# Cosine-similarity attention: values and transposes in 64-row tiles, one norm-sum set for Q and K, one product for both heads

## The chip, the cores and the metric

The kernel runs on one core of a Trainium2 chip. It uses five engines that run side by side and meet only at semaphores: TensorE (PE in the profile; its weight loads are PEld), VectorE (DVE), ScalarE (ACT), GpSimd (POOL) and SyncE (SP, which issues most transfers). Matmuls write to PSUM, a memory of eight banks. The metric is the device time of one execution in microseconds; the median of the runs counts.

## What is computed

The inputs Q, K and V have 8 batches of 12 heads, 512 positions and 64 columns, in f32; tau is 0.1.

```python
Q_norm = Q / (np.linalg.norm(Q, axis=-1, keepdims=True) + 1e-10)
K_norm = K / (np.linalg.norm(K, axis=-1, keepdims=True) + 1e-10)
scores = np.einsum('bhqd,bhkd->bhqk', Q_norm, K_norm) / tau
weights = np.exp(scores - np.max(scores, axis=-1, keepdims=True))
weights = weights / (np.sum(weights, axis=-1, keepdims=True) + 1e-10)
return np.einsum('bhqk,bhkd->bhqd', weights, V).astype(np.float32)
```

Scores of normalised rows are between -10 and 10, so the kernel leaves the maximum out and exponentiates directly.

## The kernel before

The 96 heads are worked as 48 pairs (`s`), two heads each. Every step of every pair is an `Op` with a name, an engine and a list of the names that it needs. The function `pair` creates the steps up to the transposed Q and K, `rest` those from the scores to the store, `last` the end of the last pair, `head0` the start of the first. The order on each engine is written out by hand: ORDER holds one string of step numbers for each engine, and each engine works its string from left to right. A step that needs a step of another engine waits on a semaphore, and all that stands behind it on its engine waits too.

The steps of one pair, by their names in the code:

- LD, LV: the loads of Q, K (to `qk`) and V (to `vf`), issued by SyncE. VC: GpSimd's cast of V to bf16 (`vb`), with a column of ones beside each head's 64 columns.
- SQ: squares of Q and K to `sq` (bf16), on GpSimd from the fourth pair on.
- The sums of the squares, per position and head (RED). For K, eight accumulating matmuls with an identity (SSQ, L358) fold 64 columns to 8 in columns 320 to 384 of an output bank, and VectorE reduces these 8 (L365). For Q, from the fifth pair on, VectorE reduces all 64 columns from `sq` (L369). Pairs 43 and 47 (BY_VECTOR) use VectorE for both.
- NEW: 1/sqrt of the sums by two Newton steps on VectorE (L394 to L403), for groups of one, two or four pairs (GROUPS), in a ring of three in the bank `n_ps`.
- SCL (L427): Q and K times these factors, to bf16 `qn`. Q on VectorE, K on GpSimd or, in nine pairs, on VectorE.
- TR (L433): eight transposes of 128x128 into one bank, `t_ps`: four for Q, four for K. EVA (L441): VectorE copies all eight to `qt`, where head 0 lies on rows 0 to 63 and head 1 on rows 64 to 127.
- SCO (L532): the scores of one chunk of 128 keys against 512 queries, for both heads: two matmuls of 64 rows, one on each half of the array's rows. Two buffers of two banks each (`sc_ps`) are used in turn, so the scores of a chunk wait until the exponentials of the chunk two before have been read.
- EXP (L548): ACT turns the chunk's 1024 columns into weights `et` (bf16), four chunks a pair. The first pair does it by halves (L524), the last chunk of the last pair in three pieces (L543).
- PV (L565): 32 matmuls of 128 rows and 65 columns; for each head four groups of 128 queries, each summed over the four chunks. Head 0 goes to the bank `o_ps[0]`, head 1 to `o_ps[1]`. Column 64 is the sum of the weights.
- RCP and NRM (L576, L578): reciprocal and product, per head, as soon as that head's values are complete; then ST, the store.

One chunk, the fourth of pair 43, isn't exponentiated by ACT. `poly` computes it with a polynomial on VectorE and GpSimd (OFF); its scores go to the transposes' bank.

## Time and profile before

| what | value |
|---|---|
| median of 3 runs | 190.27 us (189.93 to 191.8) |
| span of the profiled execution | 190.9 us |
| exponentials of 128x1024 on ACT | 186, busy 171.3 us |
| value matmuls | 1504, busy 72.8 us |
| score matmuls | 374, busy 73.3 us |
| transposes | 376, busy 34.3 us |
| norm-sum matmuls | 384, busy 20.0 us |

A row of a group reads: line, engine, operation, output<-input by the program's names, shapes and count; then busy time of the group in us and the mean of one in ns; then the idle time of the engine just before these instructions, and who ended it. Busy time is the union: instructions that overlap on an engine count once, so it can be less than count times mean. The chain that ended last is followed back from the last instruction, at each step to what released it. In a timeline each row is a run of equal instructions: start, length from the first start to the last end, line, operation and count.

### The profile page before, as it was taken

The numbers are of one execution on the slowest core, as the hardware profiler recorded it, in microseconds if no ns is written. First come the engines' busy times: TensorE is split into PE (matmuls) and PEld (weight loads), VectorE is DVE, ScalarE is ACT, GpSimd is POOL, SyncE is SP. The second block draws the span as 40 slices with busy tenths as digits, with TensorE's granted clock in tenths as the row PEclk, the third lists the DMA queues.
The fourth block names the chain that finished last, engine by engine and source line by source line (L and its number), as shares of the span: only waits on it lengthen the run. The fifth ranks groups of instructions, "written<-read, shape, count | busy, mean of one in ns | idle before, by whom it ended". The sixth has DMA issues, their size and how long they took to land.

```text
span 190.9 us, 6650 instructions
## 1 busy us (share of the span) xinstructions
PE 175.9 (92%) x2705; PEld 109.4 (57%) x2705; DVE 170.2 (89%) x552; ACT 182.7 (96%) x215; POOL 161.8 (85%) x150
## 2 busy tenths in 40 slices
PE   7699699999999999999999999999999899897973
PEld 2355266666656666666566666556656565464642
DVE  2668999999999999999997998999999999988642
ACT  5678999999999999999999999999999999999994
POOL 5397898999999999999999999999999994793000
PEclk9958999999999999999999999999999999999998
DMA  5999999997999599999979999999950414000565
GB/s 162 344 348 349 350 348 372 365 297 250 268 351 337 169 260 320 357 366 369 380 277 272 351 377 364 354 379 384 365 194 5 165 58 165 3 0 3 193 197 165
DMA packets 52446, 50.76 MB, mean 266 GB/s; under 512 B 3136, under 2 KB 52416, under 8 KB 52416
## 3 DMA queue, kind: packets, MB, share of 16 engines
q1 hardware_dynamic: 51984, 50.02, 79.7%
q8 instruction: 21, 0.34, 0.8%
q10 hardware_dynamic: 432, 0.33, 0.5%
q14 instruction: 9, 0.07, 0.1%
HBM read 37.75 MB, written 12.58 MB: 264 GB/s over the span
## 4 chain that ended last, share of the span: by engine, by line
ACT 89%; PE 4%; DMA 3%; DVE 1%; issue 0%; SPq 0%
ACT et L548 88%; DMA qk<-in_Q_dram 3%; PE ops L358 2%; PE scps L521 1%; PE tps L433 1%; DVE qn L427 1%; PE scps L532 0%; SPq L312 0%; ACT et L543 0%; ACT sq L333 0%; ACT ob L608 0%; PE tps L270 0%; DVE qn L261 0%; DVE ob L612 0%; PE ops L593 0%
## 5 line engine op out<-in xcount | busy, mean ns | idle before, releaser
L548 ACT ACTIVATE et<-scps 128x1024 bf16<-128x1024 f32 x186 | 171.3, 1113 | 0.6 <-PE scps L532 0.4
L341 POOL TENSOR_TENSOR sq<-qk 128x1024 bf16<-128x1024 f32 x44 | 83.1, 1896 | 0.1
L532 PE MATMUL scps<-qt 64*128 64x512 bf16 x374 | 73.3, 387 | 6.3 <-ACT et L548 3.3
L565 PE MATMUL ops<-vb,et 128*128 128x65 bf16 x1504 | 72.8, 195 | 1.7 <-DVE ob L578 1.0
L565 PEld LDWEIGHTS ops<-vb,et 128*128 128x128 bf16 x1504 | 55.3, 98 | 30.9 <-issue 18.3
L427 POOL TENSOR_TENSOR qn<-qk,rk 128x512 bf16<-128x512 f32 x38 | 39.5, 1045 | 5.9 <-PE scps L532 3.7
L578 DVE TENSOR_TENSOR ob<-ops,rd 128x256 f32<-128x256 f32 x94 | 38.8, 418 | 0.7
L427 DVE TENSOR_TENSOR qn<-qk,nps 128x512 bf16<-128x512 f32 x56 | 37.2, 677 | 0.7 <-ACT nps L386 0.6
L433 PE MATMUL tps<-ident,qn 128*128 128x128 bf16 x376 | 34.3, 222 | 0.9 <-POOL qn L427 0.3
L441 DVE COPY qt<-tps 128x1024 bf16<-128x1024 bf16 x47 | 32.1, 682 | 0.4 <-PE tps L433 0.4
L532 PEld LDWEIGHTS scps<-qt 64*128 64x128 bf16 x374 | 18.2, 92 | 23.5 <-ACT et L548 9.6
L369 DVE TENSOR_REDUCE nps<-sq 128x8 f32<-128x512 bf16 x46 | 30.8, 682 | 0.8 <-POOL sq L341 0.7
L553 POOL TENSOR_SCALAR vb<-vf 128x512 bf16<-128x512 f32 x48 | 29.7, 630 | 0.1
L433 PEld LDWEIGHTS tps<-ident,qn 128*128 128x128 bf16 x376 | 21.9, 99 | 12.0 <-issue 5.4
L576 DVE RECIPROCAL rd<-ops 128x4 f32<-128x4 f32 x94 | 16.1, 174 | 6.6 <-PE ops L565 5.9
L358 PE MATMUL ops<-sq,ident 128*128 128x64 bf16 x384 | 20.0, 199 | 0.1
L358 PEld LDWEIGHTS ops<-sq,ident 128*128 128x128 bf16 x384 | 15.2, 101 | 4.3 <-issue 2.5
L365 DVE TENSOR_REDUCE nps<-ops 128x8 f32<-128x64 f32 x46 | 10.0, 218 | 0.9 <-PE ops L358 0.7
L394 DVE TENSOR_TENSOR nps<-nps,ys 128x32 f32<-128x32 f32 (+2 forms) x34 | 7.0, 207 | 0.4
L395 DVE SCALAR_TENSOR_TENSOR nps<-nps,ys 128x32 f32<-128x32 f32 (+2 forms) x34 | 7.0, 206 | 0.4
L335 POOL TENSOR_TENSOR sq<-qk 128x512 bf16<-128x512 f32 (+1 forms) x5 | 4.7, 956 | 3.2 <-DMA qk<-in_K_dram 2.8
L524 ACT ACTIVATE et<-scps,xs 128x512 bf16<-128x512 f32 x8 | 4.9, 682 | 0.3 <-PE scps L521 0.3
(66 smaller groups left out, 57.8 us busy)
## 6 DMA issues: line engine op xcount, KB each, us to landing
vf<-in_V_dram SPq DMA_DIRECT2D x48, 256.0 KB, 6.6
qk<-in_Q_dram SPq DMA_DIRECT2D x47, 256.0 KB, 5.5
qk<-in_K_dram SPq DMA_DIRECT2D x47, 256.0 KB, 6.3
out_dram<-ob SPq DMA_DIRECT2D x47, 256.0 KB, 5.7
qk<-in_Q_dram SPq DMA_DIRECT2D x2, 128.0 KB, 2.7
qk<-in_K_dram ACTq DMA_DIRECT2D x2, 128.0 KB, 2.8
out_dram<-ob SPq DMA_DIRECT2D x1, 128.0 KB, 1.7
out_dram<-ob SPq DMA_DIRECT2D x1, 64.0 KB, 1.6
```

Source lines behind the costliest of these rows:

```text
L341: lambda e: e.tensor_tensor(out=sqf, in0=data, in1=data, op=ALU.mult))
L358: last = e.matmul(out=o_ps[bank][:, 320:384], lhsT=ident[:, :], rhs=sq[iqs][:, 8 * w : 8 * w + 8, 8 * k : 8 * k + 8], start=(k == 0), stop ...
L369: lambda e, w=w, dst=dst: e.tensor_reduce(out=dst, in_=sq[iqs][:, 8 * w : 8 * w + 8, :], axis=AX.X, op=ALU.add))
L427: lambda e, w=w, r=r: e.tensor_tensor(out=qn[iqn][:, w].rearrange("p t h d -> p h t d"), in0=qk[iq][:, w].rearrange("p h (t d) -> p h t d" ...
L433: last = e.transpose(t_ps[:, w, t, :], qn[iqn][:, w, t].rearrange("p h d -> p (h d)"), ident[:, :])
L441: lambda e: e.tensor_copy(out=qt[iqt][:, :, :, :].rearrange("p w t x -> p (w t x)"), in_=t_ps[:, :, :, :].rearrange("p w t x -> p (w t x)")))
L532: last = e.matmul(out=sc_ps[:, 2 * b + h, :], lhsT=qt[iqt][64 * h : 64 * h + 64, 1, c, :], rhs=qt[iqt][64 * h : 64 * h + 64, 0, :, :], sta ...
L548: lambda e, c=c, b=b: e.activation(out=et[iet][:, c, :, :], in_=sc_ps[:, 2 * b : 2 * b + 2, :], func=ACT.Exp, scale=math.log(2.0) / UNIT i ...
L553: lambda e: e.tensor_scalar(out=vb[:, iq, :, :, 0:DIM].rearrange("p c h d -> p h c d"), in0=vf[iv][:, :, :].rearrange("p h (c d) -> p h c ...
L565: last = e.matmul(out=o_ps[h][:, 65 * t : 65 * t + 65], lhsT=et[iet][:, c, h, 128 * t : 128 * t + 128], rhs=vb[:, iq, c, h, :], start=(c = ...
L576: lambda e, h=h, grid=grid: e.reciprocal(out=rd[io][:, h, :], in_=grid[:, :, DIM]))
L578: lambda e, h=h, grid=grid: e.tensor_tensor(out=ob[io][:, h], in0=grid[:, :, 0:DIM], in1=rd[io][:, h, :].unsqueeze(2).to_broadcast([128, N ...
```

## The change

Seven things change together, and the order of all engines is written anew.

- Transposes (`tr`): sixteen of 64 rows and 64 columns in place of eight of 128x128, alternating between the two halves of the rows; one step TR in place of two. Each half of the rows writes to a bank of its own (`turned[:, r]`). The copy EVA reads both banks and writes runs of 64.
- Values (`pv`): each matmul of 128 rows becomes two of 64, alternating between the row halves. The two of a couple belong to different heads (`h = r ^ u`) and so write to different banks; the first four steps of a pair cover one half of the sums, the next four the other. The loop runs over chunks first, so that a step needs one chunk's exponentials only. There are 3008 such matmuls. The first matmul into each bank clears it, and all others accumulate.
- Reciprocal and product: one step RCP and one step NRM for both heads. The first value step of the next pair waits for NRM of both.
- Norm sums, from the fifth pair on: one SSQ of eight matmuls with 128 columns for Q and K, into 128 columns of the second transposes' bank (`f_ps`), and one reduction to 16 values. VectorE's reductions from `sq` go.
- The norms and Newton values move from `n_ps` to the first transposes' bank (`norm`), in four slots.
- The shared banks get an order: on TensorE each of TR and SSQ waits for VectorE's reading of the one before (`frees`). On VectorE, marks "+n" in its string say between which steps the transposes of a pair may run: they wait for the last step ahead of the mark that touches the norms' bank, and the next such step waits for them (`share`).
- OFF becomes empty: ACT does all chunks, 187 exponentials of 128x1024.

```diff
+    def share(self, order, windows):
+        free = []
+        for o in order["pe"]:
+            if o.frees:
+                o.needs, free = o.needs + free, o.frees
+        last, open_ = None, []
+        for i, o in enumerate(order["dve"]):
+            for w in windows.get(i, []):
+                if last is not None:
+                    w.needs = w.needs + [last.key]
+                open_.append(w.key)
+            if o.norms:
+                o.needs, last, open_ = o.needs + open_, o, []
...
+    o_ps = nc.alloc_psum_tensor("ops", [128, 2, 512], f32)
+    nt_ps = nc.alloc_psum_tensor("ntps", [128, 2, 512], f32)
...
+                    last = e.matmul(out=f_ps, lhsT=ident[:, :], rhs=sq[iqs][:, :, 8 * k : 8 * k + 8], start=(k == 0), stop=(k == 7))
...
-            def tr(e, w=w):
-                for t in range(NT):
+        def tr(e):
+            for j in range(2 * NT):
+                for r in range(2):
+                    rows = slice(64 * r, 64 * r + 64)
                     last = e.transpose(
-                        t_ps[:, w, t, :], qn[iqn][:, w, t].rearrange("p h d -> p (h d)"), ident[:, :])
+                        turned[:, r, 64 * j : 64 * j + 64],
+                        qn[iqn][rows, j // NT, j % NT].rearrange("p h d -> p (h d)"), ident[rows, rows])
...
+        free = [("NRM", s - 1)] if s else bank_free
+        for u in range(2):
+            for i, c in enumerate(turn):
+                def pv(e, u=u, c=c, i=i):
+                    for t in range(NT):
+                        for r in range(2):
+                            rows, h = slice(64 * r, 64 * r + 64), r ^ u
+                            last = e.matmul(
+                                out=o_ps[:, h, 65 * t : 65 * t + 65],
+                                lhsT=et[iet][rows, c, h, 128 * t : 128 * t + 128], rhs=vb[rows, iq, c, h, :],
+                                start=(u == i == t == 0), stop=(u == 1 and i == NT - 1), skip_group_check=True)
...
-OFF = {(43, 3): ((43, 43), "A")}
+OFF = {}
...
-BY_VECTOR = (43, 47)
+BY_VECTOR = ()
...
-RINGS = (17, 9, 6, 4, 4, 5, 8, 3)
+RINGS = (17, 9, 6, 4, 4, 5, 8)
+SLOTS = 4
```

In the head, the new list of TensorE puts the four score matmuls of the first pair's head 0 one behind the other, ahead of the norm sums and of head 1's transpose of Q. A filler matmul of 256 columns goes. ACT's list moves one normalising exponential of the first pair ahead of the squares of the second pair's Q, and an exponential between these squares and the next.

## The prediction

> **What bounds the kernel now.** I read the page first: the shares of the engines and the chain of work that ended last.

> ```profile
> span 190.9 us, 6650 instructions
> ...
> PE 175.9 (92%) x2705; PEld 109.4 (57%) x2705; DVE 170.2 (89%) x552; ACT 182.7 (96%) x215; POOL 161.8 (85%) x150
> ...
> ACT 89%; PE 4%; DMA 3%; DVE 1%; issue 0%; SPq 0%
> ```

> Four engines are over 85% busy, but the chain lies on one of them, ScalarE (ACT). Next, the chain piece by piece (start, length, what).

> ```profile
> 18.15 116.56 ACT et L548 x127
> ...
> 134.74 22.11 ACT et L548 x24
> ...
> 156.86 10.27 ACT et L548 x11
> ...
> 167.14 11.14 ACT et L548 x12
> ...
> 178.29 7.96 ACT et L548 x9
> ...
> 186.46 0.68 ACT et L543
> ```

> From 18.15 on, the kernel is 183 exponentials one behind the other. The longest unbroken piece gives the rate: 116.56 / 127 = 0.918 us for each. At that rate 183 take 168.0 us; from 18.15 to 186.46 there are 168.3. [...] The rest of what can be won lies ahead of it, in the ACT timeline of the head:

> ```profile
> 8.40 1.24 ACT L524 ACTIVATE et<-scps,xs 128x512 bf16<-128x512 f32 x2
> 10.34 0.31 ACT L383 ACTIVATE ys<-xs,eps 128x16 f32<-128x16 f32 x1 [0.69 <-DVE xs L365]
> ...
> 14.09 0.69 ACT L524 ACTIVATE et<-scps,xs 128x512 bf16<-128x512 f32 x1 [0.31 <-PE scps L521]
> 15.18 9.49 ACT L548 ACTIVATE et<-scps 128x1024 bf16<-128x1024 f32 x10 [0.40 <-PE scps L532]
> ```

> Once the exponentials have begun, ACT idles 0.69 + 0.31 + 0.40 = 1.40 us in brackets, and no more.

> **The change, part by part.**

> *The polynomial chunk goes back to ACT.* OFF becomes empty, so the list has 187 full exponentials where it had 186. Nothing covers ACT: +0.92 us, with one answer. VectorE and GpSimd lose that chunk's arithmetic, which isn't on the chain.

> *Row tiles on TensorE.* The groups that the diff touches, and a stretch of the PE timeline:

> ```profile
> L532 PE MATMUL scps<-qt 64*128 64x512 bf16 x374 | 73.3, 387 | 6.3 <-ACT et L548 3.3
> L565 PE MATMUL ops<-vb,et 128*128 128x65 bf16 x1504 | 72.8, 195 | 1.7 <-DVE ob L578 1.0
> ...
> L433 PE MATMUL tps<-ident,qn 128*128 128x128 bf16 x376 | 34.3, 222 | 0.9 <-POOL qn L427 0.3
> ...
> L358 PE MATMUL ops<-sq,ident 128*128 128x64 bf16 x384 | 20.0, 199 | 0.1
> ```

> ```profile
> 104.21 0.40 PE L433 MATMUL tps<-ident,qn 128*128 128x128 bf16 x4
> 104.54 0.39 PE L532 MATMUL scps<-qt 64*128 64x512 bf16 x2
> 104.86 0.66 PE L565 MATMUL ops<-vb,et 128*128 128x65 bf16 x16
> 105.45 0.39 PE L532 MATMUL scps<-qt 64*128 64x512 bf16 x2
> 105.80 0.41 PE L358 MATMUL ops<-sq,ident 128*128 128x64 bf16 x8
> ```

> A run's length less one matmul's own time, over the starts between, is the pitch: values (0.66 - 0.195) / 15 = 31 ns for 65 columns, transposes (0.40 - 0.222) / 3 = 59 ns for 128, norm sums (0.41 - 0.199) / 7 = 30 ns for 64. The two score matmuls lie on 64 rows each; both together last 0.39 where one lasts 0.387, so the two row halves run at once. By the transposes' rate 512 columns need 0.24 us, yet the values start 0.32 after the scores: about 0.09 us is lost. It is lost again on the way back: the sixteenth value matmul starts at 104.86 + 0.66 - 0.195 = 105.33, the next could start at 105.36, the scores start at 105.45. So each change between 64-row and 128-row work costs some 0.09 us.

> Need of a pair before: 4 scores of 0.32 = 1.28, 4 changes into them of 0.09 = 0.36, 32 values of 31 ns = 0.99, 8 transposes of 59 ns = 0.47, 8 norm sums of 30 ns = 0.24: 3.34 us of the 4 x 0.918 = 3.67 that ACT takes. That is 91%, which fits the page's 92%.

> After, 64-row tiles carry the scores, values and transposes; only the norm sums stay at 128 rows. No trace here shows short 64-row matmuls in a row, so I bound them. Both halves at once, as with the scores: 4 scores of 0.24 = 0.95, 32 pairs of value matmuls at 31 ns = 0.99, 8 pairs of transposes at the 30 ns of 64 columns = 0.24, 8 norm sums of 128 columns at 59 ns = 0.47, two changes = 0.18: 2.83 us, 77% of ACT's time. Halves behind each other: 64 x 31 ns and 16 x 30 ns in place of the 0.99 and 0.24, 4.06 us, which is 0.39 more than ACT's 3.67. I take the first, since the score row is the one row of 64-row work there is. [...] The instruction count rises from 2705 matmuls to 4600; what isn't shown is whether they can be issued that densely for long, and that is the doubt in my chance for this.

> The 0.5 us of TensorE that a pair wins sits under ACT. It buys only the 0.3 to 0.6 us of late scores: -0.35.

> *VectorE.*

> ```profile
> L578 DVE TENSOR_TENSOR ob<-ops,rd 128x256 f32<-128x256 f32 x94 | 38.8, 418 | 0.7
> L427 DVE TENSOR_TENSOR qn<-qk,nps 128x512 bf16<-128x512 f32 x56 | 37.2, 677 | 0.7 <-ACT nps L386 0.6
> ...
> L441 DVE COPY qt<-tps 128x1024 bf16<-128x1024 bf16 x47 | 32.1, 682 | 0.4 <-PE tps L433 0.4
> L369 DVE TENSOR_REDUCE nps<-sq 128x8 f32<-128x512 bf16 x46 | 30.8, 682 | 0.8 <-POOL sq L341 0.7
> ...
> L576 DVE RECIPROCAL rd<-ops 128x4 f32<-128x4 f32 x94 | 16.1, 174 | 6.6 <-PE ops L565 5.9
> ...
> L365 DVE TENSOR_REDUCE nps<-ops 128x8 f32<-128x64 f32 x46 | 10.0, 218 | 0.9 <-PE ops L358 0.7
> ```

> Q's 46 reductions go: -30.8. The remaining 44 read 128 elements instead of 64; (682 - 218) / 448 = 1.04 ns an element makes each 285 ns: 12.5 for 10.0, +2.5. Forty-seven reciprocals of about 180 ns for 94: -7.6. Forty-seven products of 512 elements at L427's 677 ns: 31.8 for 38.8, -7.0. The transposes' copy now writes runs of 64; its 682 ns may stay, or at 1.04 ns an element reach 1.2 us, +25 at most. VectorE comes to about 127 of 170 us, 152 at the worst. All of it lies under ACT: nothing.

> *One output accumulator for both heads.* The next pair's first value matmul now waits for reciprocal and product of both heads: 0.2 + 0.18 + 0.68 us plus handovers, some 1.15 us behind the last value matmul. In the new PE list nearly always one or two chunks of scores with a norm sum or a transpose stand between, each chunk released 0.92 us after the last. In four places there is one chunk alone or little more. Behind the waiting matmul stand the next scores; I price those four places at 0.3 us at most each and take +0.3 in all. Before, this wait was per head, so it is a new one.

> *Shared banks.* Transposes, norm sums and norms lie in two banks, so transposes wait for VectorE's last touch of them, norm sums wait for the copy, and VectorE's next touch waits for the transposes. Behind a waiting transpose stand the values and scores; behind VectorE's stand its Newton steps and products. Slack at the scores:

> ```profile
> 17.72 0.39 PE L532 MATMUL scps<-qt 64*128 64x512 bf16 x2
> ```

> Scores that start at 17.72 release the exponential at 18.15, 0.43 later; a buffer is free one exponential earlier, 0.92, and exponentials overlap by about 0.1. So TensorE may be 0.35 to 0.4 us late without ACT noticing. VectorE idles a third of the time, so I price these waits at nothing; without that cover, see below.

> *The head.* Here TensorE sets the pace, and slowly. The windows for 9 to 18 us (busy time of PE, PEld, DVE, ACT, POOL, then the granted clock), and VectorE's copy for pair 2 in the timeline:

> ```profile
> 9.00:18.00 9.00, 8.93 (x98) 5.27 (x98) 6.73 (x26) 7.59 (x14) 8.64 (x8) 0.64 1.10 349
> ```

> ```profile
> 17.83 0.69 DVE L441 COPY qt<-tps 128x1024 bf16<-128x1024 bf16 x1
> ```

> PE 8.93 busy of 9.00 at a granted clock of 0.64. The new list puts the four first scores together, ahead of the norm sums, moves one normalising exponential into ACT's wait for the second pair's Q, and halves the length of the first pair's transposes. That lets pair 1 start earlier. But pair 2's scores still stand behind the copy (17.83 before), behind two Newton chains on VectorE. So the head wins between nothing and the 1.40 us of idle time, and could lose 0.5 if that copy moves back. I take -0.5, a third.

> The tail (last pair, stores) keeps its instructions: nothing.

> **Sum.** +0.92 - 0.35 + 0.3 - 0.5 = +0.4 us against the profiled 190.9: 191.3. The median of the runs is 190.27, 0.6 below the profiled span, so the forecast is 190.27 + 0.4 = 190.6. From its bounds (head -1.4 to +0.5, late scores -0.6 to 0, accumulator 0 to +1.2) it runs from about 189.2 to 192. Inside that case I lean low, 190.4, as VectorE's relief also speeds the Newton chains of the head.

> **Rivals.**

> *The head closes altogether.* All 1.40 and 0.6 us go and nothing new comes: 190.27 + 0.92 - 2.0 = 189.2; a head that keeps its full clock, run by run, might give 0.5 more, 188.7. For: TensorE is the head's bound. Against: pair 2's copy. That is as fast as ACT's work allows. Chance 0.09, a third of it beyond 1%.

> *Row halves don't overlap in short matmuls, and TensorE becomes the bound.* Fully serial: 0.39 us a pair over some 44 pairs, +17, 207. It decides from the point where the 80 matmuls of a pair start 26 ns apart on average ((3.67 - 0.95 - 0.47 - 0.18) / 80). Just under that, at 25 ns, the mean still fits (3.60 of 3.67), but the list puts up to 48 of them between two scores, 1.2 us where 0.68 plus the 0.4 of slack fit: one such place in every three or four pairs loses 0.1 to 0.4 us, so +3 to +6, 193.5 to 196.5. For it: twice the instructions. Against it: the score pairs. [...] Chance 0.14.

> *Lockstep.* TensorE and VectorE, each in order, hand two banks back and forth twice a pair. If a transpose finds VectorE still ahead of its window by more than the 0.4 us of slack, ACT stops. One tenth of a us in each of 44 pairs is +4.4: 194.8; from 0.04 us a pair (1.9 / 44) it is measurable. For: both lists are fixed and six waits a pair are new. Against: PE at 77% and VectorE at two thirds. Chance 0.18.

> **How the numbers follow.** Forecast 0.59, the head's rival 0.09, serial halves 0.14, lockstep 0.18. Range: 188.9 to 196.0; it leaves out the fastest 0.04 and the 0.12 or so beyond 196. A difference of 1% (1.9 us) is about what a measurement here can tell from none. Faster by over 1% takes the best head: 0.04. Slower: serial halves, lockstep without its mildest part and a little of the forecast's edge, 0.32. Within: 0.64.

> **What would show it.** Right: 187 exponentials at 0.918 us without breaks, PE's share near 80% with value matmuls starting in pairs some 4 ns apart and pairs about 31 ns apart, no gap between scores and values, VectorE near two thirds. Wrong: value matmuls 25 to 31 ns apart singly, or a chain that leaves ACT for PE's transposes and VectorE's copy each pair. The forecast would be wrong most easily in the head, where 0.5 us is a choice between 0 and 1.4.

## The result and the profile after

The changed kernel takes 210.84 us (median of four runs, 207.2 to 217.06) beside 190.23 for the kernel before on the same chip: a ratio of 1.094, with a 95% interval of 1.083 to 1.105. The ratio isn't the quotient of the two medians, because it leaves out two of the four executions, the profiled one among them, that took over 1.5% longer than the fastest. The profiled execution has a span of 209.6 us. It belongs to a run of 211.6 us, so it stands close to the median.

The page of the kernel after: the shares of the engines (busy time, share of the span, instructions), TensorE's granted clock and the DMA engines' busy share in 40 slices, the queue that brings instructions, the chain that ended last, and four groups.

```profile
span 209.6 us, 10353 instructions
...
PE 168.5 (80%) x4600; PEld 111.3 (53%) x4600; DVE 142.9 (68%) x407; ACT 186.0 (89%) x216; POOL 156.8 (75%) x146
...
PEclk9969999999999999999995799969988999999999
DMA  5999999950699997796499189889567967413333
...
q8 instruction: 36, 0.59, 1.3%
...
ACT 28%; PE 25%; DVE 16%; POOL 9%; DMA 9%; issue 8%; SPq 2%; POOLq 1%; DVEq 0%
...
L583 ACT ACTIVATE et<-scps 128x1024 bf16<-128x1024 f32 x187 | 174.5, 1074 | 17.1 <-PE scps L567 16.6
L374 POOL TENSOR_TENSOR sq<-qk 128x1024 bf16<-128x1024 f32 x44 | 83.1, 1896 | 15.1 <-DMA qk<-in_K_dram 14.0
...
L603 PE MATMUL ops<-vb,et 64*128 64x65 bf16 x3008 | 75.1, 193 | 10.4 <-issue 6.1
L588 POOL TENSOR_SCALAR vb<-vf 128x512 bf16<-128x512 f32 x48 | 29.5, 628 | 7.5 <-DMA vf<-in_V_dram 7.4
```

TensorE is busy 80% and VectorE 68%, close to the 77% and two thirds forecast, but partly by luck: these are shares of a span that is 19 us longer. In the last control below, with a span of 193.4 us, they are 84% and 74%. ACT now holds 28% of the chain instead of 89%, and its exponentials stood 16.6 us for scores. Two things on this page were not in the prediction. The value matmuls stood 6.1 us for "issue", that is, for nothing that the profile shows. GpSimd's squares stood 14.0 us for K's loads. The instruction queue carried 36 packets; before it was

```profile
DMA  5999999997999599999979999999950414000565
...
q8 instruction: 21, 0.34, 0.8%
```

(the DMA row is that of the kernel before, in slices of 4.8 us). Each packet is 16 KB (0.59 MB / 36). In both traces TensorE has two instructions for a matmul, a weight load (PEld) and the matmul: 2 x 4600 = 9,200 now and 2 x 2705 = 5,410 before. 36 x 256 = 9,216 and 21 x 256 = 5,376, so both traces come to some 256 instructions a packet.

Where the time went can be counted on ACT. The last full exponential ends at 205.30 us instead of 186.65. The first one starts 1.56 earlier, one more costs 0.92, and between first and last there are 23 breaks of over 0.15 us, 19.6 us in sum; before there was one, of 0.2. (A break is what an exponential ends later than 0.918 us after the one before it.) I put each break to what came before it on TensorE: 9.9 us follow a stop in the middle of a step, 7.5 follow a late load, 1.6 are the head, 0.6 other.

A stop in the middle of a step, in the PE timeline of the kernel after (start, length, what, idle time before it and its releaser):

```profile
109.01 0.23 PE L603 MATMUL ops<-vb,et 64*128 64x65 bf16 x3 [0.16 <-DVE ob L617]
111.42 0.32 PE L603 MATMUL ops<-vb,et 64*128 64x65 bf16 x5 [2.18 <-issue]
111.53 0.64 PE L567 MATMUL scps<-qt 64*128 64x512 bf16 x2
```

Three value matmuls of a group of eight run, the other five 2.4 us later, with no semaphore between. The DMA queues from 108.9 to 110.0 us (packets, MB, share of 16 engines' time) show one instruction packet among loads that fill the engines:

```profile
q1 hardware_dynamic: 391, 0.37, 101.8%
q8 instruction: 1, 0.02, 5.0%
```

That packet moved from 109.03 to 109.91. The windows show what follows (PE, PEld, DVE, ACT, POOL busy, granted clock, DMA share, GB/s):

```profile
104.00:109.00 5.00, 4.43 (x152) 2.90 (x146) 4.14 (x9) 5.00 (x6) 3.20 (x4) 1.00 0.99 315
109.10:111.40 2.30, 0.14 (x3) 0.02 (x4) 0.06 (x1) 1.05 (x2) 2.30 (x4) 0.89 1.04 353
111.40:117.00 5.60, 5.58 (x87) 3.70 (x88) 1.19 (x4) 3.11 (x4) 4.47 (x5) 0.50 0.64 221
```

In the 5.6 us after the stop the granted clock is 0.50, and ACT works 3.11 of them: the stop is paid more than once. There are eight such stops of over 0.43 us, 10.0 us in sum, and all lie at the same place in TensorE's own count of instructions: at 192 above a multiple of 256.

The late loads, in the chain from 142 to 156 us, and SyncE's list (SPq) in the timeline:

```profile
143.13 6.28 DMA qk<-in_K_dram
149.41 0.07 issue
149.48 1.35 POOL sq L374
...
155.25 0.61 PE ntps L470 x16
155.86 0.85 PE scps L567 x4
```

```profile
44.46 0.37 SPq L351 DMA_DIRECT2D vf<-in_V_dram  x1
53.12 0.38 SPq L621 DMA_DIRECT2D out_dram<-ob  x1
53.55 1.27 SPq L348 DMA_DIRECT2D qk<-in_Q_dram  x2
```

A load of K asked for at 143 lands 6.28 us later, and GpSimd squares pair 41 behind it. In GpSimd's list these squares stand ahead of the scaling of pair 36's K, so that pair 36's transposes and scores come last. At 53 us SyncE had stood 8.3 us at a store that waited for its product, with loads behind it in its list. From pair 9 on, each store of pair s stands directly ahead of V of pair s + 9 and Q, K of pair s + 12; in the list before, the stores stood among the loads of Q and K of pairs some 12 to 21 ahead. When the store goes, the loads go in a burst.

### The profile page after: what moved, and what is told of

It reads as the page before. It is cut to its first block, busy times and chain, and to the rows that moved or that the text cites. A ratio compares the mean times of both kernels' runs of the same rounds, so it can differ in the third digit from the quotient of the medians.

```text
span 209.6 us, 10353 instructions
## 1 busy us (share of the span) xinstructions
PE 168.5 (80%) x4600; PEld 111.3 (53%) x4600; DVE 142.9 (68%) x407; ACT 186.0 (89%) x216; POOL 156.8 (75%) x146
## 4 chain that ended last, share of the span: by engine, by line
ACT 28%; PE 25%; DVE 16%; POOL 9%; DMA 9%; issue 8%; SPq 2%; POOLq 1%; DVEq 0%
ACT et L583 28%; PE ops L603 8%; PE scps L567 8%; PE ntps L408 5%; DVE ob L617 5%; DMA qk<-in_K_dram 5%; POOL sq L374 4%; PE ntps L470 3%; DVE qt L478 3%; DMA qk<-in_Q_dram 3%; DVE qn L462 2%; POOL vb L588 2%; POOL qn L462 2%; DMA vf<-in_V_dram 2%; SPq L348 2%
## 5 line engine op out<-in xcount | busy, mean ns | idle before, releaser
L583 ACT ACTIVATE et<-scps 128x1024 bf16<-128x1024 f32 x187 | 174.5, 1074 | 17.1 <-PE scps L567 16.6
L603 PE MATMUL ops<-vb,et 64*128 64x65 bf16 x3008 | 75.1, 193 | 10.4 <-issue 6.1
L603 PEld LDWEIGHTS ops<-vb,et 64*128 64x128 bf16 x3008 | 62.3, 96 | 30.5 <-DVE ob L617 10.3
L478 DVE COPY qt<-ntps 128x1024 bf16<-128x1024 bf16 x47 | 32.3, 687 | 22.5 <-PE ntps L470 22.4
L462 DVE TENSOR_TENSOR qn<-qk,ntps 128x512 bf16<-128x512 f32 x56 | 36.8, 680 | 0.3
L617 DVE TENSOR_TENSOR ob<-ops,rd 128x512 f32<-128x512 f32 x47 | 32.4, 689 | 1.5 <-DVE ys L442 0.3
L408 PE MATMUL ntps<-sq,ident 128*128 128x128 bf16 x352 | 28.6, 226 | 1.2 <-DVE rd L615 0.4
L470 PE MATMUL ntps<-ident,qn 64*128 64x64 bf16 x752 | 20.4, 194 | 10.1 <-POOL qn L462 5.9
L408 PEld LDWEIGHTS ntps<-sq,ident 128*128 128x128 bf16 x352 | 20.9, 100 | 11.6 <-issue 6.5
L470 PEld LDWEIGHTS ntps<-ident,qn 64*128 64x128 bf16 x752 | 15.5, 97 | 16.6 <-issue 7.9
L388 DVE TENSOR_REDUCE ntps<-ntps 128x16 f32<-128x128 f32 x44 | 13.0, 295 | 14.9 <-PE ntps L408 14.7
L433 DVE TENSOR_TENSOR ntps<-ntps,ys 128x32 f32<-128x32 f32 (+2 forms) x34 | 7.1, 208 | 0.7
```

The source lines that it names most:

```text
L388: lambda e: e.tensor_reduce(out=dst, in_=in_, axis=AX.X, op=ALU.add)).norms = not acts
L408: last = e.matmul(out=f_ps, lhsT=ident[:, :], rhs=sq[iqs][:, :, 8 * k : 8 * k + 8], start=(k == 0), stop=(k == 7))
L462: lambda e, w=w, r=r: e.tensor_tensor(out=qn[iqn][:, w].rearrange("p t h d -> p h t d"), in0=qk[iq][:, w].rearrange("p h (t d) -> p h t d" ...
L470: last = e.transpose(turned[:, r, 64 * j : 64 * j + 64], qn[iqn][rows, j // NT, j % NT].rearrange("p h d -> p (h d)"), ident[rows, rows])
L478: lambda e: e.tensor_copy(out=qt[iqt][:, :, :, :].rearrange("p w t (r x) -> p r (w t) x", r=2), in_=turned.rearrange("p r (k x) -> p r k x ...
L583: lambda e, c=c, b=b: e.activation(out=et[iet][:, c, :, :], in_=sc_ps[:, 2 * b : 2 * b + 2, :], func=ACT.Exp, scale=math.log(2.0) / UNIT i ...
```

## The experiments

Three theories. F: TensorE's instructions come in blocks of 256, whose packets pass through DMA engines that the loads keep full (101.8% of them in the window above); 1.7 times the instructions (9,200 for 5,410) use a block up before the next is there. L: loads come late because each stands behind a store. K: TensorE and VectorE in lockstep, at the shared banks (the prediction's rival "Lockstep") or at the one output accumulator. Times are medians; each ratio is to the kernel before, with its interval.

**Values in 128-row form** (3,096 matmuls instead of 4,600; the cut is abridged):

```diff
-                        for r in range(2):
-                            rows, h = slice(64 * r, 64 * r + 64), r ^ u
-                            last = e.matmul(out=o_ps[:, h, ...], lhsT=et[iet][rows, c, h, ...], rhs=vb[rows, iq, c, h, :], ...)
+                        last = e.matmul(out=o_ps[:, u, ...], lhsT=et[iet][:, c, u, ...], rhs=vb[:, iq, c, u, :], ...)
```

> The changed kernel with its values back in matmuls of 128 rows (1504 for 3008; the first four steps of a pair are head 0, the next four head 1), everything else as changed, the order of the engines too. PE's instructions fall from 9200 to about 6200. Theory F (TensorE is starved of instructions: its stream comes in blocks of 16 KB, 256 instructions, and the changed kernel uses a block up before the next has come): the stops of 1.2 to 2.4 us in the middle of a step go, ACT's idle time of 17 us falls below 6, and the time to 191 to 196 us, though the scores pay 0.19 us for each change of form again. Theory L (SyncE's list puts each store in front of loads, so the loads come late and GpSimd, then TensorE, wait): GpSimd's 14 us of waiting for K stay, time 203 or more. Theory K (lockstep of TensorE and VectorE at the shared banks): the order is the same, PE has less slack, time 207 or more.

207.31 us, ratio 1.084 (1.075 to 1.094). Not one stop in the middle of a step is left, but the loads are as late, as its waits say (us, times, longest):

```profile
POOL sq L374 <- DMA qk<-in_K_dram: 12.5, 13, 2.9
```

ACT's breaks fall from 19.6 to 14.1 us. F's time, 191 to 196, is missed; 207.31 lies where L and K had it. So the stops go with the additional instructions, and removing them alone wins little: the loads stay late and the changes of form come back.

**Stores later** (row halves kept; from pair 8 on each store takes the place of the store four pairs later in SyncE's list, of which this is a piece, LD standing for the loads of Q and K):

```diff
- ... ST.12 LV.21 LD.24 ST.13 LV.22 LD.25 ...
+ ... ST.8  LV.21 LD.24 ST.9  LV.22 LD.25 ...
```

> The changed kernel with SyncE's list altered alone: the store of each pair from the eighth on stands where the store of the pair four later stood, so that loads are issued up to four pairs (15 us) earlier. L: GpSimd's waits for K and V (14.0 and 7.4 us) go and the time falls to 192 to 197. F: the stops in the middle of a step stay (about 10 us of PE in all), the time falls only where late loads had added to them: 199 to 205. K: no change, 207 to 211.

209.1 us (204.0 to 211.4). GpSimd's waits for loads are gone but for the first pairs; the stops grow from 8 to 12 and from 10.0 to 18.0 us. The PE timeline and the waits:

```profile
56.77 0.33 PE L603 MATMUL ops<-vb,et 64*128 64x65 bf16 x10
59.25 0.51 PE L603 MATMUL ops<-vb,et 64*128 64x65 bf16 x22 [2.15 <-issue]
```

```profile
PE ops L603 <- issue: 13.1, 10, 2.5
```

The time lies in K's range and misses F's (199 to 205) and L's (192 to 197). L alone falls: what the loads stop losing, the blocks lose. I put that down to SyncE, which now keeps the DMA engines full for longer.

**Light loads** (row halves and list kept; the output differs; abridged):

```diff
+    out=qk[iq][0 : 128 if s < R_QK else 32, w], in_=src(x, s)[0 : 128 if s < R_QK else 32]
+    out=vf[iv][0 : 128 if s < R_V else 32, :, :], in_=src(V, s)[0 : 128 if s < R_V else 32]
```

> The changed kernel with the loads of Q and K from pair 17 on and of V from pair 9 on cut to 32 of 128 partitions; the rest of each buffer keeps an earlier pair's values, so the output is another. The same instructions and orders, but a quarter of the load traffic from some 30 us on. F: a block of instructions still needs its own microsecond and more, but no longer stands behind data; the stops become fewer or shorter, time 192 to 202. L: loads land at once, though issued as late as before: 198 to 205. K: no change, 207 to 211.

197.12 us, ratio 1.029 (1.021 to 1.037), as F had it. The program on TensorE is the same to the instruction, and the stops fall to two, one of them while the loads are still whole. So the stops hang on the traffic too.

**Values in 128-row form and stores later**, both edits above:

> Both edits: values in 128 rows and stores four pairs later. F with L as its consequence: as the first, 191 to 194. L as a cause of its own: clearly below each of the two alone. K: 205 or more.

200.65 us, ratio 1.050 (1.045 to 1.056). Neither F's time (191 to 194) nor K's (205 or more) was right. It is clearly below each of the two edits alone, as L as a cause of its own had it. There is no stop and, after the first pairs, no wait for a load, and yet the time is 10 us more than before. ACT has 29 breaks, 28 of them of 0.15 to 0.4 us, 8.3 us in sum. The chain that ended last, and the longest wait, with the same wait before:

```profile
PE 42%; DVE 26%; ACT 18%; POOL 8%; issue 4%; DMA 1%; DVEq 0%
```

```profile
PEld ops L601 <- DVE ob L615: 16.5, 42, 1.0
```

```profile
PEld ops L565 <- DVE ob L578: 5.7, 17, 0.9
```

My reading: with changes of form at every change of step, 0.11 us each by the next run, TensorE has too little slack for the wait at the common accumulator. So here the waits point to the part of K that concerns the accumulator. No run takes the common accumulator out, and that the shared banks cost time as well isn't shown.

**Half the chunks' values in 128-row form**, stores later (abridged):

```diff
+                        if i % 2:
+                            last = e.matmul(out=o_ps[:, u, ...], lhsT=et[iet][:, c, u, ...], rhs=vb[:, iq, c, u, :], ...)
+                            continue
```

> Two of a pair's four chunks give their value matmuls back to 128-row form and two keep the 64-row halves; stores stand four pairs later in SyncE's list, as in the run with later stores. 7,696 TensorE instructions instead of 9,200. F (instruction blocks come too late): a block of 256 lasts 6.3 us on average instead of 5.3 us, so the stops inside steps at block boundaries, 12 with 18.0 us in the run with later stores and all row halves, become fewer: 0 to 5, under 6 us in sum; 199 to 206 us. If the row halves themselves are too slow on TensorE (serial or contending), the stops don't depend on the number of instructions and the time is half way: about 204.9 us with as many stops in the 64-row chunks as there were.

211.37 us, ratio 1.105 (1.097 to 1.113). A miss in time. The stops did as F says: none is left that a late packet explains, where there were twelve. But 63% of the chain is TensorE, and its timeline tells why:

```profile
82.84 0.29 PE L609 MATMUL ops<-vb,et 64*128 64x65 bf16 x8
83.07 0.30 PE L602 MATMUL ops<-vb,et 128*128 128x65 bf16 x4
83.30 0.30 PE L609 MATMUL ops<-vb,et 64*128 64x65 bf16 x8
83.53 0.29 PE L602 MATMUL ops<-vb,et 128*128 128x65 bf16 x4
83.75 0.39 PE L567 MATMUL scps<-qt 64*128 64x512 bf16 x2
```

Four couples take 0.12 us by themselves, and a group starts every 0.23: each change of form costs 0.11 us. My mixture changes form inside a step. From 60 to 160 us its trace has 223 changes, the 128-row form with later stores 185: 9.1 and 7.1 a pair, 0.22 us apart by that price, and the pairs are 4.06 and 3.86 us long.

**Paced loads.** All bytes and row halves; each load waits for an exponential some pairs earlier, so that transfers are spread. Three versions of the lead, and the 128-row form with the first two (abridged; D and DV are the leads in pairs):

```diff
+        for c, k in enumerate([("LD", p + D, 1), ("LD", p + D, 0), ("LV", p + DV)]):
+            P.ops[k].needs.append(("EXP", p, c if (p, c) not in OFF else c + 1))
```

> All row halves kept, all bytes moved. The loads of Q and K of pair p + 10 and of V of pair p + 5 wait for the exponentials of pair p, one load for each of its first three, and the store of pair p - 2 stands behind them: SyncE then issues four transfers spread over each pair rather than in bursts, and loads run at most 10 pairs ahead instead of 17. F with its queue (a block's packet waits 2 to 4 us behind loads when the DMA engines are full, and a block is used up in 5.3 us): from about 45 us on the engines aren't full at the request, the packet starts within about 1 us, stops inside steps fall from 12 (later stores) or 8 (the change) to 3 at most, all before 45 us, and no squares wait for a late load: 193 to 198 us. L alone (only late loads matter): the waits for loads go, the stops stay: 204 to 210 us. Instruction number alone, whatever the traffic: stops stay, 204 to 210 us. K (lockstep at the shared banks): neither moves, 205 us or more.

> Values in 128-row form in all chunks and the same paced loads: 6,192 TensorE instructions, 256 of which last 8 us. F: there was no stop to remove, and no load came late with later stores, so pacing brings nothing: 199.5 to 201.5 us, like values in 128-row form with later stores (200.65 us). If pacing helps by something other than the blocks and the late loads (less contention on the buffers), it is below 198 us here too.

232.67 and 237.45 us, ratios 1.222 (1.210 to 1.234) and 1.238 (1.225 to 1.251): both misses by my choice of V's lead. GpSimd scales V up to six pairs ahead and V was asked for five ahead, as the waits of the first show:

```profile
POOL vb L588 <- DMA vf<-in_V_dram: 40.2, 17, 6.3
```

Of the stops they say little; the first still has seven with 8.1 us, five of them after 50 us, where F had forecast none. With longer leads:

> The paced loads again with longer leads: Q and K of pair p + 13 and V of pair p + 8 wait for the exponentials of pair p. In the first paced run V came only five pairs ahead, while GpSimd scales V up to six pairs ahead, so GpSimd stood 40.2 us for V; this is mended here. All row halves and all bytes stay. F with its queue: while the rings fill, to about 55 us, the DMA engines are full and two to four stops of 1 to 1.5 us remain; after that a block's packet starts within 2 us of the request, and there is at most one stop of over 1 us. With the waits for loads under 3 us: 195 to 200 us. If the number of instructions alone makes the stops, or the queue is as full with pacing as without: 5 or more stops after 60 us and 203 us or more. If GpSimd still waits over 10 us for loads, the run says something of the stops only.

> Values in 128-row form with the same paced loads and longer leads: no stops to remove, and load waits that later stores had removed already. F and L: 199.5 to 201.5 us, as with later stores (200.65 us), so that the paced row halves come out faster than the paced 128-row form. If pacing helps through something else, such as less traffic on the buffers, both paced kernels gain alike and this one is below 198 us.

206.69 us (ratio 1.085, 1.074 to 1.097) and 200.58 us (1.053, 1.043 to 1.063). The second is as F and L say. The first misses its 195 to 200 us. Its stops moved as forecast in part: after 57 us there are three with 2.7 us, one of them over 1 us, but before, while the rings fill, six with 8.3 us, where two to four were forecast. Its DMA engines in 40 slices of 5 us:

```profile
DMA  5999999999977888999969979989858445113333
```

They are full up to 55 us, and again later: pacing spreads the bursts, but Q, K, V and the output of a pair keep the engines near full in any case.

> Paced loads once more, all row halves and all bytes kept: the lead of Q and K grows from 9 pairs to 12 and that of V from 4 to 8, so that fewer bytes are asked for before pacing begins. In the paced run with longer leads five of the six stops of over 0.5 us before 60 us were in the stretch in which the DMA engines filled the rings (7.0 us of stops, 8.6 us of late exponentials), one after it. F with its queue: the stretch is shorter, the stops between 40 and 60 us go, two to three remain before 40 us (2 to 4 us in sum); with no load later than its user the time is 195 to 201 us, below 202 us and below the paced 128-row form or equal to it. If the stops between 40 and 60 us stay though the engines are not full there, the queue is not their cause and the time is 203 us or more.

205.52 us (201.34 to 207.31). Another miss: fewer stops before 40 us (one instead of three), more after, ten with 10.7 us in all, each at a place where the DMA engines were 78% busy or more between the block's boundary and the packet. None of these versions of pacing is the cure.

**Two controls.** The kernel before with light loads, and the change with light loads and later stores:

> The kernel before with the same cut as the light loads: from pair 17 Q and K, from pair 9 V load only 32 of their 128 partitions (the rest keeps what the buffer held, so the output differs). A control: if light traffic speeds the kernel by something other than the blocks and the late loads, this one falls too, by 2 us or more. F and L: ScalarE's exponentials bound it and its blocks have 3.3 us to spare under full traffic, so nothing moves: 189.5 to 191.5 us.

> Light loads as in the run of that name (197.12 us) and the stores four pairs later as well, row halves kept; the same part of the loads is left out. GpSimd's 8 us of waits for loads, which were left there, go. Of the late exponentials (4.0 us from the third to the last) 2.0 us lay at 26 us and before, where the traffic is still full, and some 1.2 us behind waits for loads after 140 us. F and L: 195.5 to 197.5 us. Lockstep at the shared banks would leave breaks in each pair whatever the loads do, and the rate of the exponentials between 30 and 185 us would be above 0.93 us; F and L say 0.92.

The kernel before doesn't move: 190.31 us, ratio 0.999 (0.995 to 1.003). The change comes to 195.93 us, ratio 1.029 (1.020 to 1.038), also as forecast, and its chain reads like that of the kernel before:

```profile
37.77 31.32 ACT et L583 x34
```

```profile
73.82 61.75 ACT et L583 x67
```

61.75 / 67 = 0.922 us for each exponential: row halves, shared banks and one accumulator cost ACT next to nothing when instructions and data are there. K falls for this form. Its breaks over 0.15 us are six with 3.1 us, all but one before 38 us.

**The blocks in all traces.** I took every boundary of 256 TensorE instructions (192, 448, ... in its count) in seven kernels with row halves throughout: the change, later stores, both with light loads, and the paced ones. For each I compared the end of the next block's packet with the last instruction before the boundary.

```
boundaries                                                  245
packet ended later than 1.3 us before the boundary     about 77
  of these with a stop of over 0.43 us                       50
packet ended earlier, with a stop of over 0.43 us             0
from the packet's end to the next instruction, in a stop    1.0 to 1.6 us, median 1.4
```

At the 92 boundaries of the four kernels with values in 128-row form, and at the 20 of the kernel before, no packet was that late. The rates say why. With row halves a block lasts 5.0 us on average (3.4 at the shortest; from the control with light loads and later stores), in the kernel before 8.4 (7.3 at the shortest). Against it stand the packet's start after the previous boundary (median 0.8 us where the DMA engines were under 30% busy, 3.4 and up to 6.6 where they were over 90%, counted in the kernels with row halves but for that control; at most 3.7 in the kernel before), about 1 us for the packet, and 1.4 us until it is executed. That makes 3.2 us when the engines are free and, by the medians, 5.8 when they are full: row halves fit the first and not the second, and the kernel before, with 6.1 at the most, fits both.

## Why the prediction was wrong

The forecast was 190.4 us, with a range up to 196.0; the measured time is 210.84. Two terms that the sum doesn't have, late instruction blocks and late loads, stand for 17.4 of ACT's 19.6 us of breaks. A third, the head, is in the sum with the wrong sign.

**What bounds the kernel now.** Right: 183 exponentials at 0.918 us. The kernel before with light loads, which leaves the time where it was, agrees. Of the late scores' 0.6 us the profile of before shows 0.3 (168.3 against 168.0 us); the other 0.3 no run shows.

**The polynomial chunk.** Right as a term: 187 exponentials, at 0.92 us.

**Row tiles on TensorE.** The mechanism held. In the PE timeline after, 24 value matmuls last 0.54 us:

```profile
60.00 0.54 PE L603 MATMUL ops<-vb,et 64*128 64x65 bf16 x24
60.42 0.39 PE L567 MATMUL scps<-qt 64*128 64x512 bf16 x2
```

(0.54 - 0.19) / 23 = 15 ns, so a couple takes 30 ns; its halves mostly start 3 to 11 ns apart. The change of form was priced at 0.09 us and measured 0.11. The halves do overlap, so the rival of serial halves, 0.14, is out. The 4 ns that the prediction expected within a pair are near the score couples of the trace of before, whose halves start 3 to 6 ns apart. The 25 ns from matmul to matmul, at which it put the rival's lower end, was a trial value under its own 26: no run shows a limit there.

What failed is the sentence that closes this step: "what isn't shown is whether they can be issued that densely for long, and that is the doubt in my chance for this". I saw the doubt and priced it only as a pitch of matmuls, within the rival "Row halves don't overlap in short matmuls". The limit here is not the pitch but the supply: 9,200 instructions in blocks of 256, whose packets start 3.4 us after the boundary where the DMA engines are over 90% busy and 0.8 us where they are under 30% (the medians above). The page of before had both rows (21 instruction packets, and DMA engines at 9 tenths in most slices up to 140 us); I used neither. The supply had no term in the sum. In the profile after it stands for 9.9 us of breaks.

**Loads.** There was no term for them either. I followed the order of TensorE and ACT through the change and not SyncE's list, in which each store now stands directly ahead of the loads of pairs nine and twelve ahead: 7.5 us of breaks. In the 128-row form, where there are no stops, moving the stores won 6.7 us (207.31 to 200.65). With row halves the two terms feed each other: moving the stores alone won nothing beyond the spread of the runs (209.1, from 204.0 to 211.4), cutting the traffic won 13.7, and both 14.9 of the 20.6.

**VectorE.** Priced at about 127 us in work and nothing in time; its busy time is 142.9, under ACT all the same. The working took groups' busy times off the engine's, but instructions of different groups overlap: VectorE's groups add up to 203 us before, where the engine is busy for 170.2. The copy into runs of 64 takes 687 ns, so the feared +25 didn't come. Nothing in time, as forecast, outside the head, where TensorE isn't stopped and has slack.

**One output accumulator** (+0.3) **and shared banks** (nothing). Small, as forecast, with row halves: 0.922 us an exponential in the last control. In the 128-row form (200.65 us) the accumulator's wait grows, to 16.5 us, once changes of form use TensorE's slack up; I had not seen that the two parts of the change depend on each other in this way. The rival Lockstep, 0.18 at 194.8 us, meant the shared banks, and no run shows that these cost time by themselves.

**The head** (-0.5). This term has the wrong sign. ACT's timeline after:

```profile
13.62 1.95 ACT L583 ACTIVATE et<-scps 128x1024 bf16<-128x1024 f32 x2
16.01 2.14 ACT L583 ACTIVATE et<-scps 128x1024 bf16<-128x1024 f32 x2 [0.43 <-PE scps L567]
18.88 3.81 ACT L583 ACTIVATE et<-scps 128x1024 bf16<-128x1024 f32 x4 [0.73 <-PE scps L567]
```

The first full exponential starts 1.56 us sooner than the 15.18 of the profile before, and 1.58 us of breaks follow by 18.9, at pair 1's and pair 2's scores. The fifth starts at 18.88, beside 19.07 in that profile, so the head seems to win 0.2 us. But the profile before is of an execution whose head ran at a granted clock of 0.64, and its span of 190.9 us is 2.5 above 188.4, the median of the thirteen spans on record beside the two controls. The prediction took the 1.40 us of idle time in that head for the kernel's own. In the control of the kernel before, whose loads are the same up to 22 us, the clock is full and ACT has no such break (a window, then ACT's timeline):

```profile
9.00:18.00 9.00, 7.91 (x119) 4.75 (x118) 8.41 (x32) 9.00 (x15) 8.70 (x9) 1.00 1.10 355
12.67 10.19 ACT L548 ACTIVATE et<-scps 128x1024 bf16<-128x1024 f32 x11
```

There the fifth full exponential starts at 16.28. With the changed order and row halves throughout it starts at 17.6 to 17.9 in the four traces whose clock from 9 to 18 us was 1.00 as well (later stores and the three paced ones), and at 18.5 to 18.9 in the other three, whose clock there was 0.81. So the head loses 1.4 to 2.6 us, more than the 0.5 that the prediction allowed for. The prediction had named the place: pair 2's scores stand behind the copy, which starts at 14.96 in the control of the kernel before and at 16.46 with later stores:

```profile
14.96 0.69 DVE L441 COPY qt<-tps 128x1024 bf16<-128x1024 bf16 x1
```

```profile
16.46 0.68 DVE L478 COPY qt<-ntps 128x1024 bf16<-128x1024 bf16 x1
```

What is left without late blocks and late loads, 195.93 us, is 5.6 us above the kernel before on that chip (190.35). Between the traces of the two controls ACT's last full exponential ends 5.3 us apart, at 189.15 and 183.83. Of these, 2.6 are there by the fifth exponential, 0.92 is the added exponential, and 1.35 are breaks after the two stops that remain while the rings fill; the other 0.4 are one more break and the rate.

Not shown is why a packet waits 3.4 us at full engines, and when exactly it is asked for: that the request falls at the boundary is inferred from the 0.8 us at free engines. The number of instructions alone wasn't tested: no run pads the kernel before with instructions that do nothing. No version here beats the kernel before.

## What to carry to other kernels

When a change multiplies the instructions of an engine, count them against the packets of the instruction queue: here 256 a packet, used up in 5.0 us on average and 3.4 at the shortest, against 5.8 us (by the medians) from one boundary until the next block could run where the DMA engines were full. Look for stops on "issue" in the middle of a group that lie at the same place in every 256 instructions: here all 50 stood at boundaries with a late packet, fewer instructions throughout (3,096 matmuls for 4,600) removed all such stops, and less traffic six of eight. Read the DMA-issuing list along with the compute lists: here stores directly ahead of the loads of pairs nine and twelve ahead turned late products into late data, 7.5 us of ACT's breaks. Before pricing idle time in a head, compare the profile's span and its granted clock there with other executions of the same kernel.
